# One inference step of a DeltaNet and gMLP block: work off the matmul engine held behind the scan's chunk steps

## The chip, the cores and the metric

The kernel runs on one core of a Trainium2 chip. The metric is the device time of one execution in microseconds (us). The engines are called as the profile calls them: PE is the matmul engine (TensorE) and PEld its weight loads, DVE is VectorE, ACT is ScalarE, POOL is GpSimd, and SP is SyncE, whose queue issues the transfers. All five run at the same time. Each works through its own instructions in the order in which the program was built, and waits where an instruction needs something from another engine or from a transfer.

## The reference

Two sequences, a context of 128 tokens and a latent of 2048, go through one block (depth 1, width 1024):

```
proj = h @ w_in                      # q, k, v | gate | decay and beta | u | vg
o_a  = delta_bidir(q, k, v, g, beta) # gated DeltaNet, 4 heads x 128, forward and backward scan
o_a  = rmsnorm(o_a, o_norm) * silu(gate)
o_b  = gelu(u) * (w_spatial @ layernorm(gelu(vg)) + b_spatial)
x    = x + ga1 * (concat(o_a, o_b) @ w_out)
x    = x + ga2 * (square(relu(h2 @ w_ff1)) @ w_ff2)
y    = rmsnorm(x, norm_final)
```

A scan step has, for each head, `v_new = u - w S`, `o = q S + (q k^T) v_new`, `S = S * decay + k^T v_new`, where u and w come from a triangular solve that doesn't need the state S. The final states of the context are an output too.

## The kernel before

Tokens come in 17 tiles of 128: tile 0 is the context, tiles 1 to 16 the latent. There are three stages: the input projection with the convolution (to about 425 us of the profiled execution), the scan (about 425 to 1250 us), and the feed-forward part (the rest).

The scan has 34 units: two of the context (units 0 and 1), then 16 latent tiles forward (2 to 17), then the same tiles backward (18 to 33). A unit has two kinds of PE steps. Its *prep* steps solve the triangular system: a first product (L1041), then five levels, each with L1061 (product to `pd`, put into `P` by a masked copy on DVE, L1065), then L1075 and L1072 (products, copied back by ACT into `Y`, L1076, and `X`, L1077), then a last level (L1091; L1099 and L1101, which DVE and ACT copy out in L1102 and L1103), then L1109/L1110 (evicted by DVE into `R`, L1112) and L1118/L1119 (evicted by ACT into `T`, L1122). Its *chain* steps carry the state: L991 three times (with `S`, `T` and `kt`) and L1175/L1176 for the output. All these are small products, most of them in fp16 on 128x64 or 128x128, and each step waits for the copy of the one before. They are called chunk steps here.

Between them stand the *fills*, whose products are 128x512 (L221, L222, L223: three products with a high and a low part make one of full precision): in the forward half the projections `g`, `v`, `u` of the 17 tiles with gelu, layernorm statistics and so on behind them (L1210 to L1271); in the backward half, for each tile whose two directions are done, the norm of `o` (L1318 to L1326), transposes (L1339, evicted by L1342 and L1343), the product with `w_out` (L1362, L1363), and for nine tiles the second norm (L839 to L883) whose results are put in high and low parts into `hop_d` for the feed-forward part (`put`, L877 and L878).

Weights are loaded in fp32 into a staging pool of 4 buffers (`raw`), and split into a high part by ACT (L195) and a low part by DVE (L196); `load_split` does both. The 16 pieces of `w_out` are first scaled by DVE (L194) with `wscale`.

The program is built from a list of events, each a function with a time in units, sorted by time. `emit` runs them in this order. A scheduler of the framework then sets each engine's order with a timeline of its own. `emit` binds it in one place: the first PE instruction of a fill must stand behind the first PE instruction of the latest chunk step (in the backward half, of the step three before). Such a bond is one of order in the built program; it is no wait on the chip. What a fill does on DVE, ACT and POOL, and what an event without PE instructions does, is not bound.

The row of cumulated decays `g` that a unit needs first (`gb`, used by ACT in L1016) and the row `eg` that it needs last (used by DVE in L1153) share a tag with three buffers (L957 to L960).

Of the kernel before, what the change touches and what calls it, by code (L numbers as in the profile page):

```python
# [31 lines left out]
def interleave(*lists):  # L32
# [5 lines left out]
    for _, _, _, s in sorted(order, key=lambda e: e[:3]):  # L38
# [14 lines left out]
NV = 7  # L53
# [2 lines left out]
ORDER1 = (1, 5, 2, 6, 0, 7, 3, 4)  # L56
NK = DFF // P // 2
AHEAD = 3
WINDOWS = [2.46, 0.03, -0.51, 1.06, -1.61, 18.16, 17.58, 18.3,
           2.63, -0.06, -0.18, 1.0, 1.36, 1.64, 1.66, 2.66, 3.17, 3.71]  # L60

# [2 lines left out]
def hybrid_step(  # L64
# [55 lines left out]
    nhalf = cp.tile([P, 80], F32, name="nhalf")  # L120
    V.memset(nhalf, -0.5)
    zcol = edge.tile([P, 3 * KT], F32, name="zcol")[:, 0:KT]
    V.memset(zcol, 0.0)
# [39 lines left out]
    wscale = cp.tile([P, KT], F32, name="wscale")  # L163
    alog = cp.tile([P, 8], F32, name="alog")
    dtb = cp.tile([P, 8], F32, name="dtb")
    scond = cp.tile([P, KT, 2], F32, name="scond")
# [19 lines left out]
        load(out=t, in_=src)  # L186
        return t

    def split_w(raw, scale=None, pool=None, tag="w"):
# [3 lines left out]
        if scale is not None:  # L193
            V.tensor_scalar_mul(raw, raw, scale)  # L194
        A.copy(h, raw)  # L195
        V.tensor_tensor(out=lo, in0=raw, in1=f32(h), op=ALU.subtract)  # L196
        return h, lo

    def load_split(src, scale=None):
        return split_w(raw_w(src, sp, "raw"), scale)  # L200

    W2 = {"g": [], "v": [], "u": []}

    def load_w2(gi, k):
        off = {"g": 1536, "v": 2576, "u": 2064}[gi]
        W2[gi].append(load_split(w_in[0, k * P : (k + 1) * P, off : off + 512]))

    def w512(name, dt=F32):
        return wp.tile([P, 512], dt, tag="w", name=name)
# [72 lines left out]
    with ExitStack() as ph:  # L282
# [432 lines left out]
        def second_mods():  # L715

            load(out=wsT, in_=w_spatialT)
            V.tensor_copy(wscale[:, 0:4], vec[:, 68:69].to_broadcast([P, 4]))
            V.memset(wscale[:, 4:8], 0.5)
# [102 lines left out]
    def h2_steps(t, psum, tmp, wide=w512, part=None, half=None, src=None, own=None):  # L822
# [62 lines left out]
        def plain():  # L885
            put(1, u[0])
            put(2, u[1])

        def third():
            put(3, u["y"][1])  # L890
            d = part("d")
            sub(u["y"][1], u["y"][0], d)
            put(7, d)

        def fifth():
            sub(u["y"][0], u[0])
            put(5, u["y"][0])

        def sixth():
            sub(u["y"][1], u["y"][0])  # L900
            put(6, u["y"][1])

        def fourth():
            sub(u[1], u["y"][1])
            put(4, u[1])

        ops = [plain, third, fifth, sixth, fourth] if t % 2 else []
# [22 lines left out]
    with ExitStack() as ph:  # L930
# [50 lines left out]
        def unit(t, d, fresh=False, last=False):  # L981
# [9 lines left out]
                    T.matmul(p[:, h, :], lhs[:, h, :], rhs[:, h, :], start=True, stop=True)  # L991
# [33 lines left out]
            @prep.append  # L1025
            def _():
                a = u["KK"]
                for h in range(H):
                    V.scalar_tensor_tensor(out=a[:, h, :], in0=a[:, h, :], scalar=col(nbeta, h),
                                           in1=u["Es"][:, h, :], op0=ALU.mult, op1=ALU.mult)  # L1030
                G.affine_select(out=a, in_=a, pattern=[[0, 4], [1, P]], compare_op=ALU.not_equal, fill=-1.0,
                                base=0, channel_multiplier=-1)
                u["AH"], u["AL"], u["X"] = f16("AH", BA), f16("AL", BA), f16("X", BX)
                A.copy(u["AH"], a)
                V.tensor_tensor(out=u["X"], in0=u["AH"], in1=bc4(sg2), op=ALU.mult)

            @prep.append
# [251 lines left out]

        ga1 = []  # L1290

        def load_wo(n, k):
            if k == 0:
                ga1.append(wrow(mod_d[1:2, 2 * D + n * 512 : 2 * D + n * 512 + 512]))
                WO.append([])
            WO[n].append(load_split(w_out[0, k * P : (k + 1) * P, n * 512 : (n + 1) * 512], wscale[:, k : k + 1]))

        def o_loads(u):
            t = u["t"]
# [6 lines left out]
        def o_steps(du):  # L1306
# [22 lines left out]
            def trans(half):  # L1329
                def f():  # L1330
# [110 lines left out]
        for gi in "vu":  # L1441
            for k in range(NV if gi == "v" else 0, KT):
                at(-9 if gi == "v" else -8.5, lambda gi=gi, k=k: load_w2(gi, k))
        flat = flat[NF:]
        spread(p2[4], p2[5], flat, "fill")
        spread(p2[6], p2[7], [lambda n=n, k=k: load_wo(n, k) for n in range(2) for k in range(KT)], None)
# [12 lines left out]
        def emit(f, kind, lag):  # L1459

            start = len(tc.nc.cur_bb.bb.instructions)
            f()
            if kind is None or lag < 0:
                return
            pe = [x for x in tc.nc.cur_bb.bb.instructions[start:] if x.engine == mybir.EngineType.PE]
# [531 lines left out]
```

## Time and profile before

| | |
|---|---|
| time, median of 3 runs | 2627.44 us (2621.16 to 2628.88) |
| profiled execution, device time | 2625.06 us |
| its span, first to last instruction | 2623.1 us |
| PE busy | 2566.0 us (98%) |
| PEld, DVE, ACT, POOL busy | 82%, 68%, 47%, 10% |
| mean granted PE clock | 0.994 |

A row of groups gives line, engine, operation, output<-inputs, count, then busy time in us and the mean of one in ns, then the idle time of the engine just before them with what ended it. A row of the timeline gives start and duration in us, engine, line, operation, and in brackets the idle time before it and what ended it. A row of the stages gives the stretch and its length, busy us (and instructions) of PE, PEld, DVE, ACT and POOL, the granted PE clock, the busy share of the DMA engines and GB/s.

### The profile page before, as it was taken

To read this page: it belongs to the slowest core of one execution; us is meant where nothing else is said; L and a number is where in the kernel's file an instruction comes from. 1 tells how busy PE (TensorE), PEld (TensorE's weight loads), DVE (VectorE), ACT (ScalarE), POOL (GpSimd) and SP (SyncE) were. 2 spreads that over 40 slices of the span, in tenths; PEclk is the share of its full clock that TensorE was granted. 3 is DMA by queue.
4 is the path that set the end of the run, shared out by engine and by line. 5 is a ranking of instruction groups with operands and counts; after the bars stand their busy time and mean duration, and the time that the engine had idled before them with its cause. 6 is when DMAs were issued, how large, how long until landed. Compare 5 with 4: busy or idle time off the path is not lost.

```text
span 2623.1 us, 44123 instructions
## 1 busy us (share of the span) xinstructions
PE 2566.0 (98%) x15330; PEld 2150.2 (82%) x15330; DVE 1777.2 (68%) x3605; ACT 1238.7 (47%) x3086; POOL 253.4 (10%) x478
## 2 busy tenths in 40 slices
PE   8999999899999999899999999999999999999998
PEld 4899999688888778778888788888887888888887
DVE  5867745666667778786578786677675544774874
ACT  4655555555556557664245543333342432342441
POOL 3112112111112122111000000000000000000000
PEclk9999999999999999999999999999999999999999
DMA  8867637645556658896777879445369978786782
GB/s 298 285 213 220 198 110 234 217 152 163 167 167 180 191 186 246 256 281 186 279 235 236 249 229 328 146 137 152 118 204 370 338 265 281 263 255 213 237 262 94
DMA packets 533861, 579.79 MB, mean 221 GB/s; under 512 B 35500, under 2 KB 366684, under 8 KB 530054
## 3 DMA queue, kind: packets, MB, share of 16 engines
q1 hardware_dynamic: 533638, 576.98, 68.9%
q8 instruction: 120, 1.97, 0.3%
q14 instruction: 103, 0.84, 0.1%
HBM read 397.62 MB, written 179.22 MB: 220 GB/s over the span
## 4 chain that ended last, share of the span: by engine, by line
PE 81%; DMA 8%; DVE 4%; ACT 3%; issue 2%; SPq 1%; POOL 0%; DVEq 0%; POOLq 0%; ACTq 0%
PE f L221 15%; PE f L222 15%; PE f L223 15%; PE pj L221 7%; PE pj L223 6%; PE pj L222 6%; PE pd L991 3%; PE pm L221 1%; PE pm L223 1%; PE pm L222 1%; DMA r<-in_w_ff_dram 1%; PE pt L590 1%; PE pd L1176 1%; PE pd L1175 1%; DMA raw<-in_w_mod_dram 1%
## 5 line engine op out<-in xcount | busy, mean ns | idle before, releaser
L221 PE MATMUL f<-hop,zH 128*128 128x512 f32 x960 | 373.7, 390 | 2.4 <-ACT zH L1500 2.4
L223 PE MATMUL f<-hop,zL 128*128 128x512 f32 x960 | 373.6, 389 | 0.0
L222 PE MATMUL f<-hop,zH 128*128 128x512 f32 x960 | 373.2, 389 | 0.0
L221 PE MATMUL f<-hop,wH 128*128 128x512 f32 x896 | 351.7, 393 | 2.4 <-ACT x L1576 2.4
L222 PE MATMUL f<-hop,wH 128*128 128x512 f32 x896 | 349.5, 391 | 0.0
L223 PE MATMUL f<-hop,wL 128*128 128x512 f32 x896 | 344.7, 390 | 0.0
L1500 ACT CAST zH<-zraw 128x512 fp32r<-128x512 f32 x240 | 146.9, 620 | 290.8 <-DVE zraw L1494 89.4
L221 PEld LDWEIGHTS f<-hop,zH 128*128 128x128 f32 x960 | 180.2, 188 | 41.2 <-ACT zH L1500 4.0
L223 PEld LDWEIGHTS f<-hop,zL 128*128 128x128 f32 x960 | 180.2, 188 | 39.0 <-DVE zL L1494 1.7
L222 PEld LDWEIGHTS f<-hop,zH 128*128 128x128 f32 x960 | 180.2, 188 | 37.2
L1494 DVE TENSOR_TENSOR zL<-zraw,zH 128x512 fp32r<-128x512 f32 x240 | 162.7, 688 | 68.7 <-ACT zH L1500 55.9
L221 PEld LDWEIGHTS f<-hop,wH 128*128 128x128 f32 x896 | 168.8, 188 | 36.6 <-ACT x L1576 2.8
L223 PEld LDWEIGHTS f<-hop,wL 128*128 128x128 f32 x896 | 168.5, 188 | 35.6
L222 PEld LDWEIGHTS f<-hop,wH 128*128 128x128 f32 x896 | 169.0, 189 | 32.5
L223 PE MATMUL pj<-kH,wL 128*128 128x386 f32 (+2 forms) x568 | 190.5, 335 | 0.0
L221 PE MATMUL pj<-kH,wH 128*128 128x386 f32 (+2 forms) x568 | 189.1, 335 | 0.3 <-DVE kH L488 0.3
L222 PE MATMUL pj<-kL,wH 128*128 128x386 f32 (+2 forms) x568 | 189.3, 333 | 0.0
L180 POOL TENSOR_TENSOR r<-rsq,nhalf 128x1 f32<-128x1 f32 (+1 forms) x38 | 22.8, 600 | 1379.1 <-DVE rsq L179 1379.1
L1647 ACT CAST wH<-s 128x512 fp32r<-128x512 f32 x96 | 58.9, 620 | 173.0 <-DVE s L1494 173.0
L538 DVE SCALAR_TENSOR_TENSOR cv<-pj,vec,cv 128x384 f32<-128x384 f32 (+2 forms) x164 | 87.2, 539 | 58.2 <-ACT cv L535 56.8
L1065 DVE CAST_PREDICATED P<-om,pd 128x256 f16<-128x256 uint16 x170 | 71.0, 428 | 64.4 <-PE pd L1061 63.5
L221 PEld LDWEIGHTS pj<-kH,wH 128*128 128x128 f32 x568 | 107.1, 189 | 4.6 <-issue 4.2
(409 smaller groups left out, 5889.8 us busy)
## 6 DMA issues: line engine op xcount, KB each, us to landing
zraw<-z_d SPq DMA_DIRECT2D x212, 256.0 KB, 4.6
raw<-in_w_ff_dram SPq DMA_DIRECT2D x128, 256.0 KB, 4.8
hop<-hop_d SPq DMA_DIRECT2D x28, 1024.0 KB, 11.4
z_d<-c SPq DMA_DIRECT2D x96, 256.0 KB, 2.4
zraw<-s_d SPq DMA_DIRECT2D x96, 256.0 KB, 5.0
raw<-in_w_mod_dram SPq DMA_DIRECT2D x80, 256.0 KB, 4.3
r<-in_w_ff_dram SPq DMA_DIRECT2D x80, 256.0 KB, 5.3
s_d<-s SPq DMA_DIRECT2D x64, 256.0 KB, 3.2
```

What stands on the lines that cost most here:

```text
L221: T.matmul(ps, lh, rh, start=first and i == 0, stop=False, skip_group_check=more)
L222: T.matmul(ps, lh, rl, start=False, stop=False, skip_group_check=more)
L223: T.matmul(ps, ll, rh, start=False, stop=last and i == n - 1, skip_group_check=more)
L538: V.scalar_tensor_tensor(out=cv[:, o : o + m], in0=ps[:, s + sh : s + sh + m], scalar=convw[:, w, j : j + 1], in1=cv[:, o : o + m], op0=AL ...
L590: T.matmul(ps[:, i * P : (i + 1) * P], kTt[:, i * P : (i + 1) * P], rhs[:, i * P : (i + 1) * P], start=True, stop=True)
L991: T.matmul(p[:, h, :], lhs[:, h, :], rhs[:, h, :], start=True, stop=True)
L1065: V.copy_predicated(out=half(u["P"], yi), mask=half(bc4(om[s]).bitcast(U16), yi), data=pp)
L1175: T.matmul(p[:, h, :], u["qT"][:, h, :], s[:, h, :], start=True, stop=False)
L1176: T.matmul(p[:, h, :], u["QK"][:, h, :], u["vn"][:, h, :], start=s is None, stop=True)
L1494: V.tensor_tensor(out=out, in0=a, in1=b, op=op)
L1500: A.copy(h, src)
L1647: A.copy(h, s2)
```

## The change

Five things are changed in the scan.

1. `emit` now binds every DVE, ACT and POOL instruction of an event behind the first PE instruction of the latest chunk step, unless the event is itself a chunk step with PE instructions.
2. `g` gets a buffer of its own (`gr`, one buffer, in the pool that ends with prep); `eg` keeps three.
3. The pieces of `u` and of `w_out` are loaded one at a time: three ahead, and each split loads the next (`ahead`, `split_next`). The splits of `u` are spread over times -2 to -1.2, those of `w_out` over 16.4 to 18.2 units; before, `u` was loaded and split at -8.5 and `w_out` over 17.58 to 18.3.
4. `w_out` is no longer scaled. The scale goes into the eviction of the transposes: ACT's copy becomes an activation with scale, DVE's subtraction a scalar_tensor_tensor.
5. A prep step is cut in two (the copy into `AH` and the product with the mask become an event of their own), and the subtractions between the pieces that `put` stores move one event earlier.

```diff
-        def load_rows(src, t, d):
-            gb = q32("gb", 3)
+        def load_rows(src, t, d, tag, bufs, pool=None):
+            gb = q32(tag, bufs, pool)
...
-                u["gb"] = load_rows(g_d, t, d)
+                u["gb"] = load_rows(g_d, t, d, "gr", 1, pp)
...
-                u["eg"] = load_rows(eg_d, t, d)
+                u["eg"] = load_rows(eg_d, t, d, "eg", 3)
...
+            @prep.append
+            def _():
                 u["AH"], u["AL"], u["X"] = f16("AH", BA), f16("AL", BA), f16("X", BX)
-                A.copy(u["AH"], a)
+                A.copy(u["AH"], u["KK"])
                 V.tensor_tensor(out=u["X"], in0=u["AH"], in1=bc4(sg2), op=ALU.mult)
...
+        wlist = [("u", k) for k in range(KT)] + [(n, k) for n in range(2) for k in range(KT)]
+        wraw = []
+        def ahead():
+            if len(wraw) < len(wlist):
+                n, k = wlist[len(wraw)]
+                src = w2_src(n, k) if n == "u" else w_out[0, k * P : (k + 1) * P, n * 512 : (n + 1) * 512]
+                wraw.append(raw_w(src, sp, "raw"))
+        def split_next(j):
+            n, k = wlist[j]
...
+            (W2 if n == "u" else WO)[n].append(split_w(wraw[j]))
+            ahead()
...
-                    A.copy(hs, ps)
-                    V.tensor_tensor(out=ls, in0=ps, in1=f32(hs), op=ALU.subtract)
+                    scale = 0.5 if half else vec[:, 68:69]
+                    A.activation(hs, ps, AF.Copy, scale=scale)
+                    V.scalar_tensor_tensor(out=ls, in0=ps, scalar=scale, in1=f32(hs), op0=ALU.mult, op1=ALU.subtract)
...
+        for _ in range(3):
+            at(-8.5, ahead)
+        for j in range(len(wlist)):
+            at(-2 + 0.12 * j if j < KT else 16.4 + 0.12 * (j - KT), lambda j=j: split_next(j))
...
             f()
+            made = tc.nc.cur_bb.bb.instructions[start:]
+            pe = [x for x in made if x.engine == mybir.EngineType.PE]
+            if hist and not (pe and kind in ("chain", "prep")):
+                for x in made:
+                    if x.engine in COMPUTE:
+                        tc.add_manual_dep(x, hist[-1].name, mybir.DependencyInfo(
+                            mybir.DependencyClass.NoSync, mybir.DependencyReason.DATA), reason="order")
             if kind is None or lag < 0:
                 return
```

No product is added or taken away on PE: it has the same instructions in another order. On DVE the 16 scalings and two that filled `wscale` are gone. In the scan's PE order, the places where an fp16 product is followed by one on fp32 data (L221, L991, L1175 and the like) go from 277 to 400, because fills stand in shorter pieces. Lines of the changed kernel are two or three off from those before; L1061 is L1063 there, L1101 L1103, L1110 L1112, L1112 L1114, L1118 L1120.

Three places are shown. The first is ACT's order at the start of the scan, around the first copy into `Y` (L1043 before, L1045 after), which PE waits for. Before:

```order
L1034 CAST AH<-KK 128x512
L1016 ACTIVATE E<-gb,gcol 128x128 x4
L1017 ACTIVATE E<-E 128x512
L195 CAST wH<-raw 128x512 x2
L1043 CAST Y<-pd 128x512
L195 CAST wH<-raw 128x512 x2
L1241 ACTIVATE gw<-pm 128x512
L1076 CAST Y<-pd 128x128x2
```

Now:

```order
L193 CAST wH<-raw 128x512 x2
L1036 CAST AH<-KK 128x512
L1243 ACTIVATE gw<-pm 128x512
L193 CAST wH<-raw 128x512
L1045 CAST Y<-pd 128x512
L1243 ACTIVATE gw<-pm 128x512
L193 CAST wH<-raw 128x512 x2
L1078 CAST Y<-pd 128x128x2
```

One split stands between the products and the first copy where two stood, and it is one whose piece was loaded ahead; the next unit's `E` has moved behind.

The second is DVE's order in the backward half, in the unit of tile 10, from the copy of the last level into `Y` (L1102, now L1104) to the eviction into `R` (L1112, now L1114). Before:

```order
L1102 CAST Y<-pd 64x4x64
L1079 TENSOR_TENSOR QK<-QK,E 128x512
L1343 TENSOR_TENSOR oL<-pm,oH 128x512
L847 TENSOR_TENSOR ss_14387<-ss_14387 128x1
L1343 TENSOR_TENSOR oL<-pm,oH 128x512
L1112 TENSOR_TENSOR R<-pd,ident_179 128x512
```

Now:

```order
L1104 CAST Y<-pd 64x4x64
L1377 TENSOR_TENSOR x<-x,tmp 128x512
L179 TENSOR_SCALAR rsq<-r_14037 128x4
L1037 TENSOR_TENSOR X<-AH,sg_185 128x512
L1046 TENSOR_TENSOR AL<-KK,AH 128x512
L1081 TENSOR_TENSOR QK<-QK,E 128x512
L882 TENSOR_TENSOR y<-y 128x512
L1114 TENSOR_TENSOR R<-pd,ident_179 128x512
```

Ahead of `R` there now stand the next unit's `X` and `AL`, which wait for its `AH` from ACT, and a subtraction for `put`.

The third is PE's order at the same place, from L1110 to the product that uses `R` (L1118, now L1120); rows of one kind are cut to their first. Before:

```order
L1110 MATMUL pd<-Y,AL 128x128
...
L1176 MATMUL pd<-vn,QK 128x128
...
L223 MATMUL pj<-wH,oL 128x512
L221 MATMUL pj<-wH,oH 128x512
L222 MATMUL pj<-wL,oH 128x512
L223 MATMUL pj<-wH,oL 128x512
L859 MATMUL pm<-ident,x 128x128 x4
...
L1061 MATMUL pd<-Y,AH 128x64
...
L991 MATMUL pd<-S,kT 128x128 x4
...
L1118 MATMUL pd<-R,X 128x128
```

Now:

```order
L1112 MATMUL pd<-Y,AL 128x128
...
L1178 MATMUL pd<-vn,QK 128x128
...
L1043 MATMUL pd<-ident_179,X 128x128
...
L1063 MATMUL pd<-Y,AH 128x64
...
L990 MATMUL pd<-S,kT 128x128 x4
L1120 LDWEIGHTS X
L1120 MATMUL pd<-R,X 128x128
```

Sixteen fill products and four transposes stood between the two before; now there is none, only chunk steps, and the fills have moved to a later place in the unit.

More of the change, by code (lines that the diff above doesn't have):

```diff
@@ L58 @@
 AHEAD = 3
+COMPUTE = (mybir.EngineType.DVE, mybir.EngineType.Activation, mybir.EngineType.Pool)
 WINDOWS = [2.46, 0.03, -0.51, 1.06, -1.61, 18.16, 17.58, 18.3,
@@ L119, in hybrid_step @@
     V.tensor_copy(ident16, ident)
-    nhalf = cp.tile([P, 80], F32, name="nhalf")
+    nhalf = cp.tile([P, 88], F32, name="nhalf")
     V.memset(nhalf, -0.5)
@@ L162, in hybrid_step @@
     b2 = cp.tile([P, 2, KT], F32, name="b2")
-    wscale = cp.tile([P, KT], F32, name="wscale")
     alog = cp.tile([P, 8], F32, name="alog")
@@ L187, in raw_w, with split_w @@
         return t
-    def split_w(raw, scale=None, pool=None, tag="w"):
+    def split_w(raw, pool=None, tag="w"):
         h = (pool or wp).tile([P, 512], F32R, tag=tag, name="wH")
         lo = (pool or wp).tile([P, 512], F32R, tag=tag, name="wL")
-        if scale is not None:
-            V.tensor_scalar_mul(raw, raw, scale)
         A.copy(h, raw)
@@ L197, in split_w, with load_split, w2_src @@
         return h, lo
-    def load_split(src, scale=None):
-        return split_w(raw_w(src, sp, "raw"), scale)
+    def load_split(src):
+        return split_w(raw_w(src, sp, "raw"))
     W2 = {"g": [], "v": [], "u": []}
+    def w2_src(gi, k):
+        off = {"g": 1536, "v": 2576, "u": 2064}[gi]
+        return w_in[0, k * P : (k + 1) * P, off : off + 512]
     def load_w2(gi, k):
-        off = {"g": 1536, "v": 2576, "u": 2064}[gi]
-        W2[gi].append(load_split(w_in[0, k * P : (k + 1) * P, off : off + 512]))
+        W2[gi].append(load_split(w2_src(gi, k)))
     def w512(name, dt=F32):
@@ L887, in plain @@
             put(2, u[1])
+            u["d"] = part("d")
+            sub(u["y"][1], u["y"][0], u["d"])
         def third():
             put(3, u["y"][1])
-            d = part("d")
-            sub(u["y"][1], u["y"][0], d)
-            put(7, d)
+            put(7, u["d"])
+            sub(u["y"][0], u[0])
         def fifth():
-            sub(u["y"][0], u[0])
             put(5, u["y"][0])
+            sub(u["y"][1], u["y"][0])
         def sixth():
-            sub(u["y"][1], u["y"][0])
             put(6, u["y"][1])
+            sub(u[1], u["y"][1])
         def fourth():
-            sub(u[1], u["y"][1])
             put(4, u[1])
@@ L1290, in hybrid_step @@
         ga1 = []
-        def load_wo(n, k):
-            if k == 0:
+        wlist = [("u", k) for k in range(KT)] + [(n, k) for n in range(2) for k in range(KT)]
[7 more added lines that the diff above has]
+            n, k = wlist[j]
+            if n != "u" and k == 0:
                 ga1.append(wrow(mod_d[1:2, 2 * D + n * 512 : 2 * D + n * 512 + 512]))
                 WO.append([])
-            WO[n].append(load_split(w_out[0, k * P : (k + 1) * P, n * 512 : (n + 1) * 512], wscale[:, k : k + 1]))
+            (W2 if n == "u" else WO)[n].append(split_w(wraw[j]))
+            ahead()
         def o_loads(u):
```

9 lines of the change are left out of this document (2 added, 7 removed).

## The prediction

> **What bounds the kernel now.** I read the page's engines first, then the stages of the scan, then the waits of PE in time order, and at each wait the queue of the engine that released it.
>
> ```profile
> PE 2566.0 (98%) x15330; PEld 2150.2 (82%) x15330; DVE 1777.2 (68%) x3605; ACT 1238.7 (47%) x3086; POOL 253.4 (10%) x478
> ...
> 420.00:480.00 60.00, 52.62 (x306) 45.58 (x305) 28.62 (x68) 29.27 (x76) 16.85 (x7) 0.96 0.92 290
> 480.00:540.00 60.00, 58.17 (x475) 45.67 (x475) 43.14 (x127) 34.05 (x92) 10.69 (x13) 0.95 0.50 149
> 660.00:720.00 60.00, 60.00 (x520) 49.51 (x519) 36.24 (x99) 34.33 (x95) 8.96 (x11) 1.00 0.56 164
> 840.00:900.00 60.00, 54.84 (x439) 43.10 (x438) 41.67 (x113) 31.71 (x84) 8.28 (x10) 0.97 0.66 201
> 900.00:960.00 60.00, 53.86 (x470) 44.40 (x469) 47.10 (x124) 35.22 (x107) 12.59 (x15) 0.94 0.62 202
> 1020.00:1080.00 60.00, 54.69 (x480) 44.52 (x479) 48.37 (x117) 43.46 (x136) 11.42 (x13) 1.00 0.88 272
> 1080.00:1140.00 60.00, 55.02 (x473) 44.87 (x472) 47.63 (x109) 44.39 (x137) 12.49 (x16) 0.97 0.81 251
> 1140.00:1200.00 60.00, 58.00 (x510) 47.64 (x509) 46.18 (x109) 37.33 (x114) 11.38 (x13) 1.00 0.93 292
> ```
>
> PE is the bound: 98% busy, and without a gap in the forward half (660 to 720). So a gain can only come from PE's idle time and from a granted clock under 1. Both are small. Length less PE's busy time gives the idle time: 7.4 and 1.8 us at the scan's start (420 to 540), 5.2 at its middle (840 to 900), 6.1 where the directions change (900 to 960), and 5.3 + 5.0 + 2.0 = 12.3 in the backward half (1020 to 1200). One less the clock, times 60 us, is the time lost to the clock: 2.4 + 3.0 at the start, 1.8 and 3.6 around the middle, 1.8 in 1080 to 1140. Together these rows hold 32.8 us of waits and 12.6 us of clock. That is all the change can win back; what it can lose is not limited so.
>
> **The start: late splits ahead of the first copy.** ACT's rows, then PE's:
>
> ```profile
> 474.35 0.62 ACT L195 CAST wH<-raw 128x512 fp32r<-128x512 f32 x1 [2.76 <-DMA raw<-in_w_in_dram]
> 475.85 0.62 ACT L195 CAST wH<-raw 128x512 fp32r<-128x512 f32 x1 [0.89 <-DMA raw<-in_w_in_dram]
> 476.38 0.58 ACT L1043 CAST Y<-pd 128x512 f16<-128x512 f32 x1
> ...
> 477.01 0.37 PE L1061 MATMUL pd<-Y,AH 128*128 128x64 f16 x4 [5.35 <-ACT Y L1043]
> ```
>
> Two splits of `u` stand in ACT's queue ahead of the copy that PE needs, and each waits for its load. With the hold and the loads three ahead, one split stands there and its load is long issued. I take the wait off: **−5** (0, if the new place of the load is as late; −7.4, all idle time of this row). The clock around it loses 5.4, some of which belongs to the later small waits: **−3.5** (0 to −5.4).
>
> **The middle: the row of `g`.**
>
> ```profile
> ACT E L1016 <- DMA gb<-g_d: 58.5, 26, 5.9
> ...
> 889.54 0.98 ACT L1016 ACTIVATE E<-gb,gcol 128x128 f32<-128x128 f32 x3 [3.07 <-DVE P L1065]
> ...
> 891.60 0.28 PE L1061 MATMUL pd<-Y,AH 128*128 128x64 f16 x4 [3.04 <-ACT Y L1076]
> ...
> L194 DVE TENSOR_SCALAR raw<-raw,wscale 128x512 f32<-128x512 f32 x16 | 8.1, 508 | 9.4 <-DMA raw<-in_w_out_dram 9.3
> ```
>
> The first row is a wait of ACT: total us, times, longest. ACT stands 58.5 us, in 26 waits, before `E`, since `gb` takes turns with `eg` in three buffers and a buffer comes free late. Mostly PE has other work; at 891.60 it has none and waits 3.04. The row marked `<-DVE P` is one where the last release came from elsewhere, but the copy into `Y` stands behind it in the queue all the same. With `gr` apart, the buffer is free once the unit before has made its `E`, so the load has a whole unit of time. The 16 scalings of `w_out` on DVE (L194, 8.1 us, and 9.4 us of waits for loads) fall in this row too. I take **−4.5** for the waits (0 to −5.2) and **−1.5** for the clock (0 to −1.8). The scalings themselves are not on the path: PE waited there for ACT, so their own 8.1 us cost and bring nothing. The same holds for the evictions with the scale (bound: a 128x512 operation on DVE takes 683 to 820 ns in the rows further down, so +0.14 on each, beside products) as long as PE waits for `oH` from ACT: 0, up to +1. The loads are as many as before on SP's queue; with four buffers and three loads ahead, none of them holds the queue by waiting for a buffer.
>
> **The switch between kinds of products.** PE's full timeline in the gap-free forward half:
>
> ```profile
> 656.74 0.22 PE L1110 MATMUL pd<-Y,AL 128*128 128x128 f16 x1
> ...
> 656.76 0.47 PE L221 MATMUL pj<-wH,hH 128*128 128x512 f32 x1
> 657.08 0.39 PE L222 MATMUL pj<-wL,hH 128*128 128x512 f32 x1
> 657.31 0.40 PE L223 MATMUL pj<-wH,hL 128*128 128x512 f32 x1
> ```
>
> From L222 to L223 is 0.23; from L221, the first after an fp16 product, to L222 is 0.32. So a place where fp32 data follows fp16 costs 0.09. The order has 123 more of them (277 to 400), almost all in the forward half, where PE has no idle time to hide them: 123 × 0.085 = **+10.5** (8 if a third of them stand after waits or small products where the switch costs nothing; 12 at 0.095).
>
> The Trainium skill, "TensorE: Matmul & The Clock Gate", Part 2 "Step-by-step", says the contrary: weights of the next tile are loaded while the present product runs, so that a change of tile should cost nothing. The row above differs (0.32 against 0.23); by the page this term would be 0, which is a rival below.
>
> **Forward half, less cover.** Fills now stand in pieces of three between nearly every two chunk steps.
>
> ```profile
> L1065 DVE CAST_PREDICATED P<-om,pd 128x256 f16<-128x256 uint16 x170 | 71.0, 428 | 64.4 <-PE pd L1061 63.5
> L1076 ACT CAST Y<-pd 128x256 f16<-128x256 f32 x170 | 64.5, 379 | 56.5 <-PE pd L1075 56.0
> ```
>
> A piece covers 0.32 + 0.23 + 0.23 = 0.78 us, a copy takes 0.43 or 0.38, so a piece hides one copy, with about 0.35 to spare for an instruction ahead of it in the queue; a level with both, 0.81, is about even. The hold also keeps gelu and statistics (600 to 700 ns each) from slipping ahead of these copies. I take 0.1 in each of 16 units, **+1.5** (0 to +4).
>
> **Backward half, the stretch without fills.** This carries the forecast. In every second unit (22, 24, and so on) the fills now bunch in runs of up to 28 products, and from the last level to L1118 PE has chunk steps alone. Before has one such stretch, where the directions change:
>
> ```profile
> 929.80 0.22 PE L1109 MATMUL pd<-Y,AH 128*128 128x128 f16 x1
> ...
> 932.09 0.28 PE L1061 MATMUL pd<-Y,AH 128*128 128x64 f16 x4
> 932.91 0.28 PE L1061 MATMUL pd<-Y,AH 128*128 128x64 f16 x4 [0.54 <-ACT Y L1043]
> 934.85 1.16 PE L991 MATMUL pd<-S,kT 128*128 128x128 f32 x8 [1.67 <-DVE R L1112]
> 936.58 0.59 PE L1118 MATMUL pd<-R,X 128*128 128x128 f16 x4 [0.56 <-DVE o L1187]
> ...
> 939.11 0.37 PE L1061 MATMUL pd<-Y,AH 128*128 128x64 f16 x4 [0.66 <-ACT Y L1076]
> ```
>
> It costs 0.54 + 1.67 + 0.56 + 0.66 = 3.4. Now the queues of the changed order at that place:
>
> ```profile
> L1079 DVE TENSOR_TENSOR QK<-QK,E 128x512 f32<-128x512 f32 x34 | 27.9, 820 | 0.1
> L1044 DVE TENSOR_TENSOR AL<-KK,AH 128x512 f16<-128x512 f32 x34 | 23.3, 684 | 3.8 <-ACT AH L1034 3.6
> L1112 DVE TENSOR_TENSOR R<-pd,ident 128x512 f16<-128x512 f32 x34 | 23.2, 683 | 4.6 <-PE pd L1110 4.4
> L1034 ACT CAST AH<-KK 128x512 f16<-128x512 f32 x34 | 20.9, 616 | 34.9 <-POOL KK L1031 34.9
> L862 ACT ACTIVATE ev<-pm,b,a 128x128 f32<-128x128 f32 x32 | 11.9, 452 | 0.9 <-PE pm L859 0.9
> L1035 DVE TENSOR_TENSOR X<-AH,sg 128x512 f16<-128x512 f16 x34 | 14.1, 416 | 2.5 <-ACT AH L1034 2.5
> ```
>
> On ACT, four evictions `ev` (4 × 0.45 = 1.8) and `AH` (0.62) come first: 2.4. Then DVE does X (0.42), AL (0.68), QK (0.82), a subtraction for `y` (0.69, as R) and R itself (0.68): 3.3. So R is ready some 5.7 us after the stretch begins. PE meanwhile has L1109 to the output (929.80 to 932.09: 2.3) and L991 (1.16), with an L1061 between: 3.6. It waits about 2.1 at L1118, and then the copies into `P`, `vt` and `o` that stand behind R on DVE are late by about another 1.3 together: 3.4, as in the row of before. I take 3.5 for each of five stretches (units 24 to 32; lower bound 1, the two waits of 0.5 in that row; upper 6, R's 5.7 with none of PE's work ahead of it), and 0.8 for each of six odd units (0.3 to 1.5). That makes 17.5 + 4.8 = 22.3 of waits (7 to 39). What goes is among the 12.3 of before:
>
> ```profile
> 1072.50 0.62 ACT L877 CAST opH<-d 128x512 fp32r<-128x512 f32 x1 [2.76 <-DVE rsq L179]
> ...
> 1073.44 0.28 PE L1061 MATMUL pd<-Y,AH 128*128 128x64 f16 x4 [2.29 <-ACT Y L1076]
> 1122.66 0.28 PE L1061 MATMUL pd<-Y,AH 128*128 128x64 f16 x4 [1.89 <-ACT Y L1076]
> ```
>
> There the copies for `put` blocked ACT and PE waited 2.29 and 1.89; the hold moves them behind the chunk steps. So the backward half goes from 12.3 to 22.3: **+10** (−5 to +27). The stretch at 930 stays, with a little more in front of it: **+0.5** (−2 to +2). Clock: one halving costs 1.8 (1080 to 1140). The stretch at 930 stands in a row with 0.94, the wait of 2.29 at 1073 in one with 1.00, so I count two of five: **+3.6** (−1.8, the present loss gone, to +9, all five).
>
> **Sum** against the profiled execution of 2625.1: +10.5 −5 −3.5 −4.5 −1.5 +1.5 +10 +0.5 +3.6 = +11.6, so 2636.7. The median shown is 2627.4, 2.4 above that execution; the profile has the same waits whichever run it is, so I leave the sum at 2637. A measurement of this kernel tells about 0.3% (7.9 us) from no change.
>
> **Rivals.** *Faster: the stretches don't stall.* If DVE and ACT, with nothing of the fills ahead of them, reach X, AL and QK earlier than I walked (KK from POOL early; the row of L1034 shows ACT waiting 34.9 us for KK, which speaks against), R is ready when PE comes. Then all waits for queues go: +10.5, less 7.4 and 5.4 at the start, 5.2 and 1.8 in the middle, and 5.3 in the backward half (12.3 to 7): 2610.5. It decides when a stretch costs under about 1 us.
>
> *Worse.* Each stretch costs 6 and halves the clock: the backward half 39 − 12.3 = +27 and +9 in place of +10 and +3.6: 2659. The 5.9 that one wait for `gb` took shows how long a queue can stand; that PE's own steps run meanwhile speaks against.
>
> *The clock.* If only waits over about 3 us halve it (the two longest above, 5.35 and 3.04, both stand in rows under 1, the 2.29 in one at 1.00), the new order, whose waits are all under that, runs at 1 throughout: clock −12.6 in place of 3.6 − 5 = −1.4, so 2625.5. The row 900 to 960, 0.94 with no wait over 1.67 shown, speaks against. The Trainium skill, the same page, Part 1, has such a rule: the clock halves after an idle window of about 3.4 us. By it the time would be this rival's; the trace agrees at 477 and 891 and differs at 930.
>
> *Switches are free.* If the 0.09 is hidden where a piece stands beside a wait anyway, the sum is 2637 − 10.5 = 2626.
>
> **Chances.** Forecast 0.40 (own range 2622 to 2650; three quarters of it over +0.3%), faster 0.28, worse 0.14, clock 0.10, free switches 0.08. Over 0.3% slower: 0.29 + 0.14 = 0.43. Faster: 0.28 and 0.02 from the lower ends of the last two: 0.30. Between: 0.11 + 0.16 = 0.27. From 2609 to 2658 leaves out about half of the worse case and a third of the faster one, under 2 in 10.
>
> **What the profile after would show.** Right: no wait of ACT for the `g` row; PE idle under 3 us in 460 to 480; the mean of L221 in the scan up, as its followers start later; PE waits of 1 to 2.5 us at L1118 for R, with L1061 late behind it, once in every second backward unit; PE busy without a gap at 660 to 720. Wrong: backward stages with under 7 us of idle time (then the faster rival), a clock of 1.00 throughout (the clock rival), or forward units no longer than before (free switches). A load of `u` or `w_out` that is late in its new place would undo the first two gains.

## The result and the profile after

| | before | changed |
|---|---|---|
| median | 2627.76 us (4 runs) | 2643.01 us (2640.55 to 2643.66, 4 runs) |
| ratio | | 1.0063 (95% interval 1.0048 to 1.0077) |
| span of the profiled execution | 2623.1 us | 2641.3 us |
| PE busy | 2566.0 us | 2580.7 us |

The change costs 15 us, a little more than the 11.6 of the sum. The profiled executions differ by 18.2. The page's engines, changed kernel:

```profile
PE 2580.7 (98%) x15330; PEld 2150.1 (81%) x15330; DVE 1769.5 (67%) x3587; ACT 1240.1 (47%) x3086; POOL 254.8 (10%) x478
```

Its stages of the scan:

```profile
420.00:480.00 60.00, 55.95 (x333) 48.63 (x332) 26.13 (x61) 25.22 (x69) 13.55 (x4) 1.00 0.92 292
480.00:540.00 60.00, 57.41 (x463) 43.45 (x463) 42.59 (x125) 35.52 (x96) 10.56 (x13) 0.97 0.51 151
660.00:720.00 60.00, 58.95 (x495) 46.80 (x494) 35.98 (x95) 32.04 (x87) 8.11 (x10) 1.00 0.52 157
840.00:900.00 60.00, 60.00 (x513) 48.64 (x512) 44.60 (x118) 36.21 (x96) 8.99 (x11) 1.00 0.61 191
900.00:960.00 60.00, 53.67 (x495) 44.85 (x494) 45.67 (x119) 38.25 (x116) 12.28 (x14) 0.94 0.75 244
1020.00:1080.00 60.00, 55.19 (x478) 45.51 (x478) 45.43 (x106) 40.89 (x124) 10.37 (x12) 1.00 0.80 242
1080.00:1140.00 60.00, 56.23 (x481) 46.18 (x479) 44.73 (x105) 44.56 (x141) 12.41 (x15) 0.97 0.87 264
1140.00:1200.00 60.00, 53.24 (x455) 44.80 (x455) 47.93 (x113) 37.99 (x116) 12.94 (x14) 0.94 0.88 272
```

PE has the same 15330 products and is busy 14.7 us longer: the loss is only in part idle time. At the start and in the middle (840 to 900) idle time has gone (7.4 to 4.1, and 5.2 to 0); in 1140 to 1200 it has grown from 2.0 to 6.8. The stretch 660 to 720, without a gap before, now has 1.05 of idle time and 495 products instead of 520.

Where the 18.2 came from is read off one product that every unit has, the one that uses `R` (L1118, now L1120). PE's timelines, before and then changed, for units 2, 16, 20 and 33:

```profile
550.50 0.39 PE L1118 MATMUL pd<-R,X 128*128 128x128 f16 x4
...
855.37 0.39 PE L1118 MATMUL pd<-R,X 128*128 128x128 f16 x4
...
955.10 0.40 PE L1118 MATMUL pd<-R,X 128*128 128x128 f16 x4
...
1246.93 0.40 PE L1118 MATMUL pd<-R,X 128*128 128x128 f16 x4
```

```profile
549.93 0.40 PE L1120 MATMUL pd<-R,X 128*128 128x128 f16 x4
...
867.36 0.33 PE L1120 MATMUL pd<-R,X 128*128 128x128 f16 x3
...
954.22 0.28 PE L1120 MATMUL pd<-R,X 128*128 128x128 f16 x2
...
1262.85 0.33 PE L1120 MATMUL pd<-R,X 128*128 128x128 f16 x3
```

The forward half (unit 2 to 16) takes 317.4 instead of 304.9, **+12.6**; the middle (16 to 20) 86.9 instead of 99.7, **−12.9**; the backward half (20 to 33) 308.6 instead of 291.8, **+16.8**. The scan starts 2.2 later and gains 2.7 by unit 2; what follows unit 33 takes 2.2 more.

The same stretches as rows of the stages (the first begins with the scan's first product), before and then changed:

```profile
471.26:550.50 79.24, 70.02 (x577) 55.20 (x577) 52.82 (x147) 41.54 (x107) 12.60 (x16) 0.94 0.56 172
550.50:855.37 304.87, 304.28 (x2654) 253.23 (x2652) 201.91 (x567) 173.23 (x470) 54.33 (x68) 1.00 0.57 167
855.37:955.10 99.73, 88.43 (x739) 70.77 (x736) 72.60 (x187) 55.34 (x156) 16.57 (x20) 0.95 0.66 212
955.10:1246.93 291.83, 279.37 (x2421) 229.44 (x2420) 217.17 (x504) 188.90 (x587) 54.13 (x63) 0.99 0.74 229
```

```profile
473.42:549.93 76.51, 69.87 (x569) 52.74 (x569) 51.16 (x145) 43.19 (x112) 12.46 (x16) 0.98 0.55 167
549.93:867.36 317.43, 313.77 (x2655) 248.27 (x2655) 203.45 (x567) 171.98 (x461) 53.33 (x68) 1.00 0.53 160
867.36:954.22 86.86, 80.81 (x710) 66.46 (x708) 65.50 (x164) 55.34 (x155) 16.68 (x19) 0.96 0.73 237
954.22:1262.85 308.63, 286.23 (x2432) 236.63 (x2429) 219.13 (x517) 191.44 (x599) 58.97 (x66) 0.98 0.70 217
```

Of the forward +12.6, 9.5 is busy time of PE (304.28 to 313.77) and 3.1 idle time (0.6 to 3.7). In the backward half the idle time grows by 9.9 (12.5 to 22.4). The middle does not hold the same work in both kernels: in the changed one 18 of the wide products with `w_out` and eight transposes fewer start there, and 20 more wide products start behind unit 33. At 0.23 and 0.11 us each in the trace of before, that is about 5 us (an estimate), so about 8 of the −12.9 is a gain for the same work.

The next table has the stages' figures for the kernels that settle the causes.

### The profile page after: what moved, and what is told of

It is laid out like the page before. It is cut to its first block, busy times and chain, and to the rows that moved or that the text cites. A ratio compares the mean times of both kernels' runs of the same rounds, so it can differ in the third digit from the quotient of the medians.

```text
span 2641.3 us, 44133 instructions
## 1 busy us (share of the span) xinstructions
PE 2580.7 (98%) x15330; PEld 2150.1 (81%) x15330; DVE 1769.5 (67%) x3587; ACT 1240.1 (47%) x3086; POOL 254.8 (10%) x478
## 4 chain that ended last, share of the span: by engine, by line
PE 81%; DMA 7%; DVE 6%; ACT 3%; issue 2%; SPq 0%; POOL 0%; DVEq 0%; POOLq 0%; ACTq 0%
PE f L222 15%; PE f L224 15%; PE f L223 15%; PE pj L222 6%; PE pj L224 6%; PE pj L223 6%; PE pd L990 3%; PE pm L222 2%; PE pm L224 2%; PE pm L223 2%; DMA raw<-in_w_mod_dram 1%; DMA r<-in_w_ff_dram 1%; PE pd L1178 1%; PE pd L1177 1%; PE pt L591 1%
## 5 line engine op out<-in xcount | busy, mean ns | idle before, releaser
L222 PE MATMUL pj<-wH,hH 128*128 128x512 f32 x240 | 111.2, 463 | 0.0
```

Of the source, the lines that this page charges most:

```text
L222: T.matmul(ps, lh, rh, start=first and i == 0, stop=False, skip_group_check=more)
```

## The experiments

Each kernel was timed beside the kernel before, whose median was between 2623.7 and 2625.5 in these comparisons (2627.8 in that of the changed kernel). "Stages" are the changes against before in the profiled execution: forward (unit 2 to 16), middle (16 to 20), backward (20 to 33). "Switches" are the places of the forward half at which a product on fp32 data follows an fp16 one, counted in the built order. The profiled executions of 3 and 11 lie 8 and 5 us under their medians, so their stages are read for where time went, not for how much in all. In the kernels with the hold in the backward half (changed, 2, 4, 7, 9 and 10) the middle lacks the 18 wide products, about 4 us of its figure.

| kernel | median | against before: ratio (95%) | switches | forward | middle | backward |
|---|---|---|---|---|---|---|
| changed | 2643.0 | 1.0063 (1.0048 to 1.0077) | 239 | +12.6 | −12.9 | +16.8 |
| 1 spacing only | 2654.0 | 1.0106 (1.0090 to 1.0121) | 240 | +19.8 | +2.7 | +8.8 |
| 2 respaced | 2654.7 | 1.0108 (1.0092 to 1.0124) | 127 | +0.1 | −8.9 | +39.7 |
| 3 no hold | 2621.4 | 0.9982 (0.9972 to 0.9992) | 239 | +10.9 | −8.4 | −4.3 |
| 4 hold only | 2675.7 | 1.0188 (1.0170 to 1.0205) | 127 | +0.1 | +5.3 | +44.2 |
| 5 no cut, no hold | 2602.4 | 0.9913 (0.9900 to 0.9926) | 129 | −0.8 | −9.3 | −3.0 |
| 6 no cut, hold forward | 2605.5 | 0.9924 (0.9911 to 0.9937) | 127 | +0.1 | −6.9 | −9.5 |
| 7 respaced, prep free | 2627.3 | 1.0009 (1.0000 to 1.0018) | 129 | −0.8 | −11.8 | +14.5 |
| 8 row of g only | 2608.1 | 0.9938 (0.9927 to 0.9950) | 129 | −0.5 | −7.1 | −7.1 |
| 9 forward at 17 | 2630.0 | 1.0012 (1.0003 to 1.0022) | 127 | 0.0 | −12.3 | +16.2 |
| 10 changed, prep free | 2633.0 | 1.0023 (1.0013 to 1.0034) | 239 | +10.9 | −14.9 | +8.5 |
| 11 weights only | 2629.9 | 1.0012 (1.0002 to 1.0021) | 127 | −0.3 | −4.1 | +4.3 |
| 12 row of g and put | 2603.8 | 0.9920 (0.9906 to 0.9934) | 129 | −0.4 | −7.0 | −6.9 |

**1. Spacing only.** The built order shows that the 112 added switches don't come from the hold: without it there are as many. They come from part 5. An 18th prep step makes the places of all steps in a unit finer, and they fall otherwise between the fills.

```diff
-            n = len(u["prep"])
-            for j, st in enumerate(u["prep"]):
+            n = len(u["prep"]) + 1
+            for j, st in zip([0, 1] + list(range(3, n)), u["prep"]):
                 at(i - w[0] + (j + 0.5) * (w[0] - w[1]) / n, st, "prep")
```

> The kernel before, in which the prep steps of a unit are only placed as if there were one more of them (the times of 18 steps instead of 17, with an empty place after the second); no work is moved between steps, nothing is held. In the built order this alone takes the places of the forward half where a product on fp32 data follows an fp16 product from 127 to 240 (239 in the changed kernel). Theory A, the loss of the forward half is this switch, 0.085 us each, and comes from the finer spacing of the prep steps: 2627.8 + 113 x 0.085 = 2637 (2634 to 2641), with PE busy nearly all of the time in 600 to 840. Theory B, the loss comes from the hold (work off PE that is late): 2628 (2624 to 2631).

Measured 2654.0: slower than both theories said. That the spacing alone costs time is shown, against B. The forward half loses 19.8, not A's 9.6, but 9.7 of it are waits (PE's idle time there is 10.3, in before 0.6); the other 10.1 are busy time of PE, about what A said. ACT's timeline at one of the waits, then PE's:

```profile
792.82 1.28 ACT L1016 ACTIVATE E<-gb,gcol 128x128 f32<-128x128 f32 x4 [5.12 <-DMA gb<-g_d]
794.00 0.35 ACT L1093 CAST Pm<-pd 64x256 f16<-64x256 f32 x1
...
794.41 0.19 PE L1099 MATMUL pd<-Pm,X 64*64 64x64 f16 x1 [2.01 <-ACT Pm L1093]
...
862.36 0.19 PE L1099 MATMUL pd<-Pm,X 64*64 64x64 f16 x1 [1.47 <-ACT Pm L1093]
```

Here `g` still shares its buffers: ACT stands 5.12 for its row, ahead of the copy into `Pm`, and with shorter pieces as cover PE waits too. Kernels 3, 5 and 9, where `g` has its own buffer, price the switch without these waits.

**2. Respaced.** All five parts, but the steps at the old places.

```diff
-            n = len(u["prep"])
-            for j, st in enumerate(u["prep"]):
+            n = len(u["prep"]) - 1
+            for j, st in zip([0, 1, 1.5] + list(range(2, n)), u["prep"]):
```

> The changed kernel with all five parts, but the prep steps are placed at the times of before (the new step, which has no product, half way between its neighbours), so that the forward half has 127 switches again; the backward half has 170 (164 in the changed kernel, 155 before). Theory A: 2643.0 - 112 x 0.085 - about 2.5 of the small forward waits = 2631 (2627 to 2635). Theory B: 2643 (2640 to 2646).

Measured 2654.7, a miss for both. The forward half did what A said (+0.1), and the backward half lost 39.7. There PE stands still at the first product of nearly every unit. POOL's, ACT's, DVE's and PE's timelines at one of them:

```profile
1064.36 0.64 POOL L1030 TENSOR_SCALAR_AFFINE_SELECT KK<-KK 128x512 f32<-128x512 f32 x1 [1.00 <-DVE r L1335]
...
1067.33 1.16 ACT L861 ACTIVATE ev<-pm,b,a 128x128 f32<-128x128 f32 x3 [1.27 <-PE pm L858]
1068.37 0.62 ACT L1036 CAST AH<-KK 128x512 f16<-128x512 f32 x1
...
1068.24 1.58 DVE L1377 TENSOR_TENSOR x<-x,tmp 128x512 f32<-128x512 f32 x1
1069.75 0.68 DVE L1081 TENSOR_TENSOR QK<-QK,E 128x512 f32<-128x512 f32 x1
1070.35 0.41 DVE L1037 TENSOR_TENSOR X<-AH,sg 128x512 f16<-128x512 f16 x1
...
1070.82 0.40 PE L1043 MATMUL pd<-ident,X 128*128 128x128 f16 x4 [2.94 <-DVE X L1037]
```

KK is ready at 1065.0, but `AH` starts only at 1068.4, behind evictions `ev` of a fill, and `X` stands behind two more operations on DVE: the step that PE waits for is held with the rest.

**3. No hold.**

```diff
-            if hist and not (pe and kind in ("chain", "prep")):
+            if False:
```

> The changed kernel without the hold on DVE, ACT and POOL work; all else as changed, so the forward half has 239 switches. Theory A: the forward loss of some 10 us stays, the uncovered stretches of the backward half go (about -8): 2636 (2630 to 2642). Theory B: all that the hold costs goes, the gains of the row of g and of the loads stay: 2618 (2613 to 2623).

Measured 2621.4, within B, but in two parts: the forward half keeps its loss (+10.9), as A said, and the backward loss goes (−4.3 where the changed kernel has +16.8; even if all 8 us by which this execution lies under its median stood there, most of the loss would be gone). So the two losses of the changed kernel have two causes.

**4. Hold only.** `emit` as changed, all else as before.

> The kernel before with the hold alone; 127 switches in the forward half, 172 in the backward half (155 before). Theory A: the forward half as before, backward +17 x 0.085 = +1.4 and the stretches' waits of some +5, less 5 for the copies that no longer stand behind fills: 2629 (2623 to 2636). Theory B: the whole loss is here, 2643 (2638 to 2650).

Measured 2675.7, worse than either said. The forward half is unharmed (+0.1), the backward half loses 44.2, with waits for `X` of 2.3 to 4.3 in every unit as in 2. Of the parts that were run alone (1, 4, 8 and 11) the hold is the costliest. In the changed kernel `AH` and `X` have a full place between them and their product, in 2 half a place; the two differ in nothing else but the spacing, and that takes the backward loss from 39.7 to 16.8.

**5. No cut, no hold.** The old prep step and no hold; `gr`, the loads, the unscaled weights and the moved subtractions stay.

> The changed kernel without the hold and with the prep step uncut, so with the row of g apart, the loads one at a time, the weights unscaled and the subtractions moved. Forward half 129 switches (127 before, 239 changed), backward half 156. Theory C (the forward loss is the finer spacing's switches, about 0.1 us each with what waits come with them; the backward loss is the hold): the kernel without the hold (2621.4) less its forward loss of 11 = 2610 (2605 to 2616). Theory D (what the coarser spacing gains in the forward half it loses in the backward half, as in the respaced kernel): 2621 (2617 to 2628).

Measured 2602.4, beyond C (2605 at best) and against D. It differs from 3 in the cut alone: 19 us in the medians, and 11.7 in the forward half of the profiled executions. This version beats both kernels: 0.9913 (0.9900 to 0.9926) of before, some 40 us under the changed one.

**6. No cut, hold in the forward half only.** As 5, with `time < NT + 1 and` ahead of the hold's condition.

> As the kernel without cut and without hold, but with the hold for events of the forward half alone. Theory C, in which the hold costs only where PE has stretches without fills: within 5 of the kernel without hold, 2612 (2606 to 2618), with PE busy all the time in 600 to 840. Theory D: the hold costs wherever it stands, 2630 or more.

Measured 2605.5, just under C's range; against 5 no difference can be told (the intervals overlap). In the forward half, where PE always has fills, the hold is nearly free.

**7. Respaced, prep free.** As 2, but the hold leaves all prep and chain steps out.

```diff
-            if hist and not (pe and kind in ("chain", "prep")):
+            if hist and kind not in ("chain", "prep"):
```

> The changed kernel with the prep steps at the times of before (as in the respaced kernel, 2654.7), but those prep steps that have no product (E, KK, AH and X) are not held; fills and the rest still are. Theory E, the waits of 2.3 to 3.9 us at the first product of twelve backward units come from the hold on the step that makes AH and X itself: they vanish, and with them the half clock behind them: 2654.7 - 12 x 2.8 + 6 = 2627 (2619 to 2634). Theory F, X is late since the queue ahead of it holds late fill work, whatever is held: 2650 (2644 to 2658).

Measured 2627.3, on E's number; F falls. The waits for `X` are gone (the longest left at that product is 0.34). That the number fits is partly chance: idle time in the backward half fell by 11.6 only (36.2 to 24.7), since other waits came (5.7 in all at L1120, for `o` from DVE), and much of the rest is the granted clock, 0.94 in 2 and 0.99 here. The hold's condition took prep steps without products for work that PE doesn't wait for, and that alone cost 27 us here. The backward half still loses 14.5 (3.0 gained without any hold, in 5).

**8. Row of g only.** Part 2 of the change alone.

> The kernel before with nothing but a buffer of its own for the row of g. Theory G, ACT's 58.5 us of waits for that row cost PE the wait of 3.04 at 891.6 and some of its clock: 2625.05 - 3 - 1.5 = 2621 (2617 to 2624). Theory H, ACT only waits elsewhere: 2625 (2623 to 2628).

Measured 2608.1, far under G's 2621. ACT's waits for the row, of before and then of this kernel (total, times, longest):

```profile
ACT E L1016 <- DMA gb<-g_d: 58.5, 26, 5.9
```

```profile
ACT E L1016 <- DMA gr<-g_d: 7.5, 2, 6.1
```

It gains 7.1 in the middle and again 7.1 in the backward half, where in before ACT stood in 10 waits for the row, 20.7 us in all. Which of PE's small waits hung on which of these was not traced.

**9. Forward at 17.** The changed kernel, in which context and forward units alone have the old places.

```diff
+            if i <= NT:
+                n = len(u["prep"]) - 1
+                js = [0, 1, 1.5] + list(range(2, n))
+            else:
+                n = len(u["prep"])
+                js = list(range(n))
```

> The changed kernel with the prep steps of the context and forward units alone at the times of before; the backward units keep the finer spacing, and all is held as in the changed kernel. Forward half 127 switches (239 changed), backward 158 (164 changed). Theory A, the forward loss is the switches and the short pieces alone: 2643.0 - 112 x 0.1 = 2632 (2629 to 2636), PE without a gap in 600 to 840, the same loss in the backward half. Rival: the forward spacing shifts work into the next stretch and the gain is lost by the end: 2643 (2639 to 2646).

Measured 2630.0, 13.0 under the changed kernel, where A gave 11.2. Every other stage stays: forward 0.0 instead of +12.6, middle −12.3 (−12.9), backward +16.2 (+16.8). Products of the forward half by shape (600 to 840; mean of one in ns), changed and then this kernel:

```profile
L222 PE MATMUL pj<-wH,hH 128*128 128x512 f32 x115 | 54.1, 470 | 0.0
```

```profile
L222 PE MATMUL pj<-wH,hH 128*128 128x512 f32 x116 | 51.5, 444 | 0.0
```

The first of the three products of a fill takes 470 ns on the mean where it took 444 (443 before), as more of them stand behind an fp16 product. Between units 2 and 16 the traces have 194 switches in the changed kernel and 100 before, and PE's busy time is 9.5 us longer, 0.10 for each of the 94 (17 of the other added ones stand before unit 2). In 1, 3 and 10, which have as many switches, it is 314.1 to 314.4 there, and here 304.4, with 0.5 of idle time. So the forward loss is shown to be the finer spacing: 9.5 of the switches, and 3.1 of waits.

**10. Changed, prep free.** The changed kernel with the edit of 7.

> The changed kernel with its finer spacing, in which the prep steps without products (E, KK, AH and X) are not held; fills and the rest are. Theory E, the hold costs through these steps in the changed kernel too (its waits of about 2.2 for P in every second backward unit stand behind a late KK on DVE): 2643 - 15 = 2628 (2622 to 2633). Rival, with the step cut they have time enough, and the 22 that the hold costs come from held fills and stores: 2642 (2638 to 2646).

Measured 2633.0, the upper end of E: the backward half loses 8.5 instead of 16.8. By the medians, 10.0 of the 21.6 us that the hold costs here are its effect on the prep steps; the rest (2633.0 to 2621.4 without the hold) is the hold on fills and on the other events without products. Which of these was not tried.

**11. Weights only.** Parts 3 and 4 alone.

> The kernel before with the weights part alone: loads one at a time, three ahead, u and w_out split at their new times, w_out unscaled. By the difference of two kernels run before (g row alone 2608, and with weights and subtractions 2602.4) it is worth 5.7: 2619 (2616 to 2623), most of it at the scan's start. Rival: at the start the wait for a late load is only exchanged for another, and the 5.7 are the subtractions of the second norm in the backward half: 2625 (2622 to 2628).

Measured 2629.9, a miss for the first theory: by the interval a trace slower than before. The profiled execution gains 4.1 in the middle and gives 4.3 back in the backward half; why it does wasn't settled.

**12. Row of g and put.** Part 2 and the moved subtractions.

> The kernel before with the row of g in a buffer of its own and the subtractions of the second norm one event earlier, without hold, without cut, with the weights as before. The g row alone gave 2608.1, g row, weights and subtractions together 2602.4, the weights alone +4 against before. If the 5.7 between the first two are the subtractions: 2602 or, with the weights' loss gone, 2598 (2595 to 2604). If they come from the weights, which then only pay beside a free ACT queue: 2608 (2605 to 2611).

Measured 2603.8, between the two numbers. Its interval overlaps with that of 8 and with that of 5, so whether the subtractions or the weights make up the 5.7 between those two stays open. Either is small beside the row of `g`.

## Why the prediction was right, and where it wasn't

**The switch and the cover in the forward half** (+10.5 and +1.5, together 12.0): measured 12.6, and 12.6 went again when only the spacing was taken back (9). The sum was right, its parts less so: 123 places at 0.085 stood for what were 94 places in this stage at 0.10 (9.5), and the waits were 3.1, twice the cover's 1.5. Of the work that the hold was to keep back here, gelu's ACT operations take some 600 ns, but the statistics only 280 and 157. Where the short pieces come from I hadn't asked: not from the hold, but from the count of prep steps, which sets all their places. The rival in which the switch is free is out. The Trainium skill ("TensorE: Matmul & The Clock Gate", Part 2, "Step-by-step") has a tile's weights loaded while the product before it runs; by that alone a switch should cost nothing, and the 0.10 us measured here differs. Why it costs this was not tried.

**The start** (−5 and −3.5): by the rows of the stages the idle time of 420 to 540 went from 9.2 to 6.6, −2.6, and the clock's loss from 5.4 to 1.8, −3.6. In time only 2.7 of the 8.5 came by unit 2, as much as the idle time; PE's busy time there stayed (70.0 and 69.9), so the clock's part is not seen in it. The step that failed is "the load is long issued, so the wait goes". The load is in time, but ACT's queue now stands before another transfer (ACT's rows, then PE's):

```profile
477.38 0.60 ACT L1243 ACTIVATE gw<-pm 128x512 f32<-128x512 f32 x1 [2.94 <-DMA gate_d<-gw]
477.87 1.13 ACT L193 CAST wH<-raw 128x512 fp32r<-128x512 f32 x2
478.90 0.37 ACT L1078 CAST Y<-pd 128x256 f16<-128x256 f32 x1
...
479.33 0.28 PE L1063 MATMUL pd<-Y,AH 128*128 128x64 f16 x4 [2.85 <-ACT Y L1078]
```

The activation writes to a buffer `gw` whose store to `gate_d` hasn't ended; the copy for PE stands behind it. The wait of 5.35 became one of 2.85, and a new one came: 2.17 at 490.66, where the next unit's first product waits for `X`.

**The middle** (−4.5, −1.5 and +0.5, together −5.5): measured −12.9, about −8 for the same work; the kernels that keep that work in the middle have −7.1 (8), −8.4 (3) and −9.3 (5). The mechanism was right, the size too small. I counted the one wait at 891.60 and the clock of its row; the row of `g` alone brings 7.1 here and 7.1 more in the backward half, which I hadn't counted at all (8). The error was to price 58.5 us of ACT's waits by the one long wait of PE that the timeline names; that smaller waits behind other releasers hung on it too is argued from 8. The faster rival didn't happen: its 2610.5 is passed only by kernels without the finer spacing and without the backward hold (5, 6, 8 and 12), so not by stretches that bear the hold without a stall.

**The backward half** (+10 and +3.6, together 13.6): measured +16.8, with 9.9 more of idle time from unit 20 to 33. In the rows 1020 to 1200, for which the +10 was worked out, it is only 3.0 (12.3 to 15.3). Stretches without fills do stall once in every second unit, at 1043.42, 1092.69, 1142.22 and 1191.81, by 2.0 to 2.3. But the place is another: not L1120 for `R`, where no wait over 0.3 is left, but L1074 for `P`, some 5 us earlier. PE's and DVE's timelines at the first:

```profile
1040.22 0.28 PE L1063 MATMUL pd<-Y,AH 128*128 128x64 f16 x4
...
1043.42 0.29 PE L1074 MATMUL pd<-P,X 128*128 128x64 f16 x4 [2.20 <-DVE P L1067]
```

```profile
1038.81 1.24 DVE L851 TENSOR_SCALAR x<-x,r 128x512 f32<-128x512 f32 x2
1039.98 0.68 DVE L1155 TENSOR_TENSOR qT<-qT,eg 128x512 f32<-128x512 f32 x1
1040.58 1.13 DVE L1028 SCALAR_TENSOR_TENSOR KK<-KK,nbeta,Es 128x128 f32<-128x128 f32 x4
1041.63 0.68 DVE L1376 TENSOR_TENSOR tmp<-pj,row 128x512 f32<-128x512 f32 x1
1042.23 0.20 DVE L1335 TENSOR_TENSOR r<-r,oss 128x4 f32<-128x4 f32 x1
1042.36 0.68 DVE L1166 TENSOR_TENSOR S<-pd,se 128x512 f32<-128x512 f32 x1
1042.95 0.41 DVE L1067 CAST_PREDICATED P<-om,pd 128x256 f16<-128x256 uint16 x1
```

The products for `P` are done by 1040.5; the copy starts at 1042.95, behind two long scalings of a fill, the chain's `qT`, the next unit's `KK`, a fill's `tmp` and the chain's `S`. So the reading was right in kind: work of fills and of the next unit lands in front of the copies of a stretch that has nothing else for PE. But I walked the queues from the last level on, as if DVE stood empty there; it had come in with the scalings still to do, so the wait fell earlier, and while PE stood at L1074 ACT and DVE caught up (the last is argued, not shown).

Over the whole backward half PE's waits for `P` from DVE are (total, times, longest) in before, the changed kernel and the one without the hold (3):

```profile
PE pd L1072 <- DVE P L1065: 1.1, 2, 0.6
```

```profile
PE pd L1074 <- DVE P L1067: 12.0, 9, 2.3
```

```profile
PE pd L1074 <- DVE P L1067: 5.2, 3, 2.1
```

So the hold makes most of these waits (with the prep steps exempt, in 10, they are 4.2), but not all: three, of 2.1, 1.6 and 1.4, each two units after the other, stay without it. Another 4.7, in seven waits, is PE waiting for `oH` at the start of a fill (1.0 without the hold); the prediction allowed at most +1 for that eviction. So the idle time came near the +10 partly by luck: the rows that the +10 was worked out for hold only 3.0 of it, and other waits make up the rest.

**The clock** (+3.6 in the backward half): the granted clock of 1020 to 1200 is 1.00, 0.97 and 0.94, 5.4 us lost against 1.8 before, so +3.6. That number fits by luck: two halvings at 1.8, less the 1.8 of before that the range takes off too, would have been +1.8, and by these rows there were three. The rival in which no wait under 3 us halves the clock is out: the longest wait of 1140 to 1200 is 2.26, at 1142.22, and the row has 0.94. The Trainium skill (the same page, Part 1) puts the halving behind an idle window of about 3.4 us; here waits of 2.2 were followed by a halving in one row and by none in another (1020 to 1080: 2.20, clock 1.00). The wait of 3.04 at 891 in before, which the prediction counts as agreeing with that rule, is under 3.4 too.

The sum by stages: 12.6 − 12.9 + 16.8 − 2.7, with 2.2 before the scan and 2.2 behind it, gives 18.2. Of the signs named in advance, ACT's waits for the `g` row were gone, and the mean of L221 went up; but the idle time of 460 to 480 was 4.05, not under 3; 660 to 720 was not without a gap; and the waits stood at another line. The middle's gain was forecast too small (−5.5 for −12.9), the backward loss too small (13.6 for 16.8) and the start's gain too large (−8.5 for −2.7); these errors partly cancel, so that the total came within 4 of the median's difference is in part luck.

## What to carry to other kernels

A rule that holds back "work off the bound engine" must know which of that work the bound engine waits for next: here steps without products fed the first product of the next unit, and exempting them was worth 27 us (2 against 7) and 10 us (changed against 10). A cut that adds a step to an evenly spaced list moves all the others; compare the built order with the cut alone before charging a loss to the part that looks heavier. And a buffer shared by an early and a late tenant can cost far more than the waits of the bound engine that carry its name: 58.5 us of ACT's waits at the head of its queue were worth 17 us of the total.

## What was not expected

The same hold cost 51 us alone (4), 22 on top of the other four parts (changed against 3), and nothing that can be told in the forward half alone (6 against 5). And a place where an fp32 product follows an fp16 one costs about 0.1 us of PE time (9.5 us for 94 of them), which no idle time shows, since PE counts as busy throughout.
